# A two-layer decoder trunk: the FFN's up products summed in PSUM chains with operands from one half of SBUF, and f's sums of the down projection made by adding transfers

## The chip, the cores and the metric

The kernel runs on one core of a Trainium2 chip. The time is the device time of one execution in microseconds (us). TensorE (PE) multiplies, VectorE (DVE), ScalarE (ACT) and GpSimd (POOL) do elementwise work, SyncE (SP) and the other queues issue transfers. A matmul here takes a stationary 128x128 operand and a moving 128x512 operand from SBUF and adds into a PSUM bank of 128x512 float32.

## The reference

Two layers, each a token mixer of three groups (MLA, GLA, RWKV-7) and a gated ConvFFN, on a sequence of 1024 tokens of width 1024:

```python
def conv_ffn(h, w_up, conv_w, conv_b, w_down):
    u = jnp.einsum('bsd,df->bsf', h, w_up)
    u = lax.conv_general_dilated(u, conv_w[:, None, :].astype(u.dtype), window_strides=(1,),
                                 padding=[(CONV_WIDTH - 1, 0)],
...
    gate, val = u[..., :D_FF], u[..., D_FF:]
    return jnp.einsum('bsf,fd->bsd', jax.nn.silu(gate) * val, w_down)

for l in range(DEPTH):
    h = rms_norm(x, ln1_g[l])
    p = jnp.einsum('bsd,dp->bsp', h, w_in[l])
...
    x = x + jnp.einsum('bsm,md->bsd', y, w_out[l])
    x = x + conv_ffn(rms_norm(x, ln2_g[l]), ffn_w_up[l], ffn_conv_w[l], ffn_conv_b[l], ffn_w_down[l])
return rms_norm(x, final_g)
```

The lines left out make y from p by the three mixers. D_FF is 2816, so the up projection makes 2 x 22 tiles of 128 rows (22 of gate, 22 of value), and the down projection reads f = silu(gate) * val in 22 tiles.

## The kernel before

Every float32 operand is held as two parts, a high one that ACT rounds and a low one that DVE or POOL subtracts (`split`, L1270); `mm3` (L97 issues) makes three matmuls of such a pair. Both FFN projections use a 2x2 block scheme with seven products in place of eight.

**Up projection.** For each j of 22 (one gate tile and one value tile) there are seven products p = 1, 2, 6, 5, 3, 7, 4, each 12 matmuls of 128x512 (four blocks k, three matmuls each): 1848 matmuls per layer. The stationary operand of a product is an item: `up_item` (L1354) builds the four weight sums (tiles S12, S34, on POOL after the first j's) and splits the chosen part into the tile `wr`, which lives in one of seven left slots, `RING`. The moving operands are the tokens' block sums: B11 (p=1), B21 (2), T2 (6), T1 (5), B22 (3), T3 (7), T4 (4). B11 to B22 lie in the pool `bp` and T3 in `wp`, both on the right side of SBUF; T4 (tiles T_m1, T_kb00 and so on) in left slots. So all products but p=4 take the weights from the left and the tokens from the right. `product` (L1482) gives each product its own bank, by turns from `aps` and `bps` (tiles psa and psr). `evac` (L1448) empties each bank: ACT copies p=1 and 5, DVE adds a copied term for 2, 6, 3, 7 and 4, and POOL adds the last term to the gate's and the value's second half. Then `taps` (L1439) applies the three conv taps to the gate (ug) and the value (uv): one ACT instruction and two DVE instructions of 1023 and 1022 columns, all from SBUF to SBUF; ACT makes the SiLU, DVE multiplies gate and value, and f[j] is stored to DRAM (`fdr`).

**Down projection.** 11 q's (two tiles of f and of w_down each, loaded as the eight quarters of `R`, L1523) in groups of 3, 4 and 4. Each q has seven products in the order 1, 2, 5, 6, 3, 7, 4, summed over the q's of a group in PSUM: 924 matmuls per layer. Before products, DVE makes the sums of f's quarters (R[0..3]) and of the weights' quarters (R[4..7]) in four steps, sum_a to sum_d (L1551 to L1564), and splits (`down_split`, L1568; ACT the high, DVE the low part) into `de` units; `down_product` adds each finished bank to an accumulator (L1604 wide, L1607 narrow).

**Around them.** The out projection (w_out rows k = 0 to 7, `wout_w`) runs before the up projection, tile of tokens by tile; its weights are split into left slots except k = 7. `up_norm` (L1274) turns each token tile into B11, B21 (first four tiles) or B22, T1, T2, T3 (last four). The order on each engine is set by a scheduler from the order of the code, so every engine runs its queue in a fixed order.

## Time and profile before

| | |
|---|---|
| median of 3 runs | 2751.63 us (2751.45 to 2755.01) |
| profiled execution, own time | 2754.38 us |
| its span in the profile | 2752.6 us |
| mean granted TensorE clock | 0.974 of full speed |
| PE busy | 2650.9 us, 96% of the span, 13586 matmuls |
| DVE busy | 1867.2 us (68%) |
| POOL busy | 1125.0 us (41%) |
| ACT busy | 1080.8 us (39%) |

The profiled execution is 2.8 us above the median. Stretches below are counted in us from the start of the span. Layer 1's out projection starts near 590, its up projection near 690 and its down projection near 1155; layer 2 repeats these places some 1372 us later. A matmul's listed duration overlaps the next one's; the pace is read from start to start. The granted clock of a window is its mean over the window, of the two levels 1.2 and 2.4 GHz (0.5 and 1.0).

### The profile page before, as it was taken

The page shows a single profiled execution, that of the slowest core. Times are in us where ns is not written, and L with a number is a line of the kernel's source. Part 1 is how long each engine was busy: PE and PEld are TensorE (multiplying, and loading weights), DVE is VectorE, ACT ScalarE, POOL GpSimd, SP SyncE. Part 2 cuts the span into 40 slices and gives each one's busy share as a digit, 9 for nine tenths or more (in the row PEclk, how much of TensorE's full clock was granted, in tenths as well). Part 3 has the DMA queues.
Part 4 walks back from the last instruction along what each step waited for, and adds up shares of the span by engine and source line. Part 5 has one row for each costly group of instructions (what it writes and reads, how often), then busy time and mean ns, then how long its engine had stood idle before and what let it go on. Part 6 is the DMA issues. An engine that isn't in the chain of part 4 may idle for free. (4 is left out here: it accounts for less than half of the span.)

```text
span 2752.6 us, 35450 instructions
## 1 busy us (share of the span) xinstructions
PE 2650.9 (96%) x13586; PEld 2135.5 (78%) x13586; DVE 1867.2 (68%) x2470; ACT 1080.8 (39%) x1764; POOL 1125.0 (41%) x915
## 2 busy tenths in 40 slices
PE   8999999999899999999899999999998999998998
...
GB/s 128 31 31 62 64 61 38 45 126 138 52 86 77 84 77 77 237 100 101 58 45 31 31 70 73 51 32 57 121 135 54 77 81 81 80 74 260 85 84 62
DMA packets 237050, 224.11 MB, mean 81 GB/s; under 512 B 39288, under 2 KB 187216, under 8 KB 236880
## 3 DMA queue, kind: packets, MB, share of 16 engines
...
## 5 line engine op out<-in xcount | busy, mean ns | idle before, releaser
L97 PE MATMUL psb<-hh,wh 128*128 128x512 f32 (+2 forms) x704 | 267.3, 381 | 6.5 <-ACT acc L748 3.8
L1443 DVE SCALAR_TENSOR_TENSOR acc<-ug,convc,acc 128x1023 f32<-128x1023 f32 x88 | 190.6, 2166 | 122.2 <-ACT acc L1441 122.1
L97 PE MATMUL psb<-hl,wh 128*128 128x512 f32 (+2 forms) x704 | 270.7, 385 | 0.8 <-DVE hl L208 0.8
L97 PE MATMUL psb<-hh,wl 128*128 128x512 f32 (+2 forms) x704 | 270.1, 384 | 0.8 <-POOL wl L258 0.8
L97 PE MATMUL psa<-B,wr_m 128*128 128x512 f32 x744 | 187.7, 402 | 1.9 <-DVE uv L1471 1.9
L97 PE MATMUL psr<-B,wr_m 128*128 128x512 f32 x744 | 185.6, 397 | 0.0
L97 PEld LDWEIGHTS psa<-B,wr_m 128*128 128x128 f32 x744 | 142.6, 192 | 37.5 <-DVE uv L1471 2.7
L254 POOL TENSOR_TENSOR ws<-ws,pcol 128x1024 f32<-128x1024 f32 x36 | 70.4, 1958 | 243.0 <-DMA ws<-in_w_in 242.8
L97 PEld LDWEIGHTS psr<-B,wr_m 128*128 128x128 f32 x744 | 140.6, 189 | 34.2 <-DVE s_va L1460 0.3
L97 PEld LDWEIGHTS psb<-hh,wh 128*128 128x128 f32 (+1 forms) x704 | 132.9, 189 | 36.5 <-issue 4.9
L97 PEld LDWEIGHTS psb<-hh,wl 128*128 128x128 f32 (+1 forms) x704 | 133.2, 189 | 33.3 <-issue 10.5
L97 PEld LDWEIGHTS psb<-hl,wh 128*128 128x128 f32 (+1 forms) x704 | 133.1, 189 | 29.2 <-issue 5.4
L258 POOL TENSOR_TENSOR wl<-ws,wh 128x1024 fp32r<-128x1024 f32 (+1 forms) x40 | 91.0, 2276 | 105.9 <-ACT wh L256 70.9
L1441 ACT ACTIVATE acc<-ug,convc 128x1024 f32<-128x1024 f32 x44 | 54.8, 1246 | 202.1 <-POOL ug L1466 202.1
L1443 DVE SCALAR_TENSOR_TENSOR acc<-uv,convc,acc 128x1023 f32<-128x1023 f32 x88 | 120.0, 1364 | 8.0 <-ACT acc L1441 6.7
L1272 DVE TENSOR_TENSOR wr_m<-wu_m,wr_m 128x512 fp32r<-128x512 f32 x88 | 120.9, 1375 | 0.2 <-ACT wr_m L1271 0.2
L1272 POOL TENSOR_TENSOR wr_sg<-S_va,wr_sg 128x512 fp32r<-128x512 f32 x40 | 58.0, 1449 | 120.0 <-ACT wr_sg L1271 116.3
L1468 ACT ACTIVATE acc<-acc 128x1024 f32<-128x1024 f32 x44 | 46.7, 1062 | 149.1 <-DVE acc L1443 149.1
L1271 ACT ACTIVATE de_m<-R 128x1024 fp32r<-128x1024 f32 x59 | 61.9, 1052 | 109.9 <-PE psb L97 50.8
L1364 POOL TENSOR_TENSOR S_va<-wu_m 128x512 f32<-128x512 f32 x42 | 57.0, 1358 | 114.8 <-issue 107.6
L256 ACT ACTIVATE wh<-ws 128x1024 fp32r<-128x1024 f32 (+2 forms) x44 | 43.7, 993 | 150.7 <-PE psb L97 141.4
L97 PE MATMUL psb<-de 128*128 128x512 f32 x348 | 94.6, 394 | 0.0
...
## 6 DMA issues: line engine op xcount, KB each, us to landing
...
```

Source lines behind the costliest of these rows:

```text
L97: pe.matmul(o, lhsT=l, rhs=r, start=first, stop=last, skip_group_check=on)
L254: eng.tensor_tensor(ws, ws, g.rearrange("p (k o) -> p k o", o=1).to_broadcast([128, K, M]), ALU.mult)
L256: act.activation(wh, ws, AF.Copy)
L258: eng.tensor_tensor(wl, ws, wh.bitcast(F32), ALU.subtract)
L1271: act.activation(d[0], s, AF.Copy)
L1272: eng.tensor_tensor(d[1], s, d[0].bitcast(F32), ALU.subtract)
L1364: eng.tensor_tensor(X[:, 0], v[:, 0:4], v[:, 4:8], ALU.add)
L1441: act.activation(a, u, AF.Identity, scale=conv[:, 2, jj:jj + 1], bias=conv[:, 3, jj:jj + 1])
L1443: dve.scalar_tensor_tensor(a[:, d:T], u[:, 0:T - d], conv[:, 2 - d, jj:jj + 1], a[:, d:T], ALU.mult, ALU.add)
L1468: act.activation(a, a, AF.Silu)
```

## The change

- **Chains.** P6 adds onto P1's bank, P7 onto P6's, P4 onto P7's, and P3 onto P5's; P2 has its own. Between them ACT copies the bank's state out for p = 1, 6, 5 and 4, DVE adds once for p = 2, 7 and 3, and POOL's two adds are gone. From j = 3 on the taps' result stands in PSUM (`bigps`) and not in SBUF. The final product gate * val is made in two halves, the first with a factor of -1, so that f's first half is stored negated and f's sums in the down projection become additions.
- **Halves.** Items of p = 2, 6, 5, 7 and 3 live in five slots RG on the right side, beside B21, T2, T1, B22 and T3; items of p = 1 and 4 in three left slots, beside B11 (moved to left slots kb01, kb11, va01, va11) and T4. The rows k = 5 and 6 of w_out take RG in place of those left slots, and the first token tile's out projection does k = 0 to 4 of both halves first.
- **Small moves.** `raw` has two buffers, the subtraction of B11 from a token tile is four DVE instructions of 256 columns in place of two of 512, and p = 7 comes before p = 3.
- **Down projection.** For q in the second and third group f's sums are made by adding DMAs on the POOL queue (`plus`, 64 in all, 128x512 each); DVE keeps the weights' sums. In the first group the low parts of p = 1 are split by POOL. The finished banks are subtracted.

```diff
-            if k < 7:
+            if k < 5:
                 woh[k], wol[k] = (slot(o, [128, D], F32R, "wo") for o in WOA[k])
+            elif k < 7:
+                woh[k], wol[k] = (RG[:, 2 * k - 10 + n].rearrange("p a k c -> p (a k c)") for n in range(2))
...
-        B11, B21, T2, T1, B22 = (pair(n) for n in ("B11", "B21", "T2", "T1", "B22"))
+        RG = bp.tile([128, 5, 2, 4, 128], F32R, tag="RG", name="RG")
+        B21, T2, T1, B22 = (pair(n) for n in ("B21", "T2", "T1", "B22"))
+        B11 = [[slot(t, [128, 2, 512], F32R, "B11") for t in ts] for ts in (("kb01", "kb11"), ("va01", "va11"))]
...
+        def less(x, tk):
+            for part in B11:
+                for n in range(2):
+                    xn = x[:, 2 * n:2 * n + 2]
+                    dve.tensor_tensor(xn, xn, part[n][:, :, tk].bitcast(F32), ALU.subtract)
...
-        RING = ("m4", "m5", "sg", "m9", "m8", "kb11", "m3")
+        RING = ("m4", "m5", "sg")
...
-            c = slot(RING[rn % len(RING)], [128, 2, 4, 128], F32R, "wr")
+            n = made[up]
+            c = RG[:, (n + 4) % 5] if up else slot(RING[n % 3], [128, 2, 4, 128], F32R, "wr")
...
-            if p == 2:
+            if p in (1, 5, 6):
+                act.activation(s[:, {1: 0, 5: 1, 6: 2}[p]], ps, AF.Copy)
+            elif p == 2:
                 tmp[j, "g"] = wp.tile([128, T], F32, tag="wl", name="ug")
                 dve.tensor_tensor(tmp[j, "g"][:, H0], ps, s[:, 0], ALU.add)
-            elif p == 6:
-                dve.tensor_tensor(s[:, 2], ps, s[:, 0], ALU.add)
-            elif p == 5:
-                act.activation(s[:, 1], ps, AF.Copy)
+            elif p == 7:
+                tmp[j, "v"] = wp.tile([128, T], F32, tag="wl", name="uv")
+                dve.tensor_tensor(tmp[j, "v"][:, H1], ps, s[:, 1], ALU.add)
             elif p == 3:
                 u = tmp[j, "g"]
                 dve.tensor_tensor(u[:, H1], ps, s[:, 2], ALU.add)
-                pool.tensor_tensor(u[:, H1], u[:, H1], s[:, 1], ALU.add)
-                a = tmp[j, "a"] = taps(u, j, dict(tag="x", bufs=2))
-                act.activation(a, a, AF.Silu)
+                a = tmp[j, "a"] = xr.tile([128, T], F32, tag="x", name="acc", bufs=2)
+                act.activation(a, taps(u, j, a if j < 3 else bigps()), AF.Silu)
+            else:
+                u = tmp[j, "v"]
+                act.activation(u[:, H0], ps, AF.Copy)
+                b = taps(u, NF + j, lp.tile([128, T], F32, tag="raw", name="b", bufs=2) if j < 3 else bigps())
                 a = tmp[j, "a"]
+                dve.scalar_tensor_tensor(a[:, H0], a[:, H0], -1.0, b[:, H0], ALU.mult, ALU.mult)
+                dve.tensor_tensor(a[:, H1], a[:, H1], b[:, H1], ALU.mult)
                 nc.sync.dma_start(out=fdr[j], in_=a)
...
+            elif p == 2 or p == 5:
+                banks[j, p] = banks["big"][:, H1] if (j, p) == (2, 2) else bps()
+            else:
+                banks[j, p] = banks[j, {6: 1, 7: 6, 4: 7, 3: 5}[p]]
+            ps, new = banks[j, p], p in (1, 2, 5)
             c = items.pop((j, p))
             for k in range(4):
-                mm3(ps, (c[:, 0, k], c[:, 1, k]), rhs(p, k), k == 0, k == 3)
+                mm3(ps, (c[:, 0, k], c[:, 1, k]), rhs(p, k), new and k == 0, k == 3, not new)
...
+        def plus(o, x):
+            pool.dma_start(out=o, in_=x, accum_op=ALU.add)
+
+        def sum_a(R, q):
+            if q in groups[0]:
+                dve.tensor_tensor(R[:, 2], R[:, 2], R[:, 3], ALU.add)
+            else:
+                plus(R[:, 2], fdr[2 * q + 1][:, H1])
+                plus(R[:, 0], fdr[2 * q][:, H1])
+            dve.tensor_tensor(R[:, 6], R[:, 4], R[:, 6], ALU.subtract)
+
+        def sum_b(R, q):
+            if q in groups[0]:
+                dve.tensor_tensor(R[:, 2], R[:, 2], R[:, 0], ALU.add)
+            else:
+                plus(R[:, 2], fdr[2 * q][:, H0])
+                plus(R[:, 1], R[:, 2])
+            dve.scalar_tensor_tensor(R[:, 6], R[:, 6], -1.0, R[:, 7], ALU.mult, ALU.subtract)
...
-            split(dent[q, p], two(draw[q], *OPS[p]), dve)
+            split(dent[q, p], two(draw[q], *OPS[p]), pool if p == 1 and q in groups[0] else dve)
```

sum_c and sum_d follow the same pattern: on DVE, f's part for the first group only, and one 128x512 instruction for the weights.

**Place 1: PE in the middle of layer 1's up projection.** psa and psr are banks, the numbers buffers. Before, one j's products stand one behind the other (P1, P2, P6, P5, P3, and P7's first matmul), each in a bank of its own:

```order
L97 MATMUL psr_8559<-B11_4913,wr_m4_8429 128x512 x12
L97 MATMUL psa_8577<-B21_4914,wr_m5_8447 128x512 x12
L97 MATMUL psr_8595<-T2_4915,wr_sg_8470 128x512 x12
L97 MATMUL psa_8618<-T1_4916,wr_m9_8487 128x512 x12
L97 MATMUL psr_8635<-B22_4917,wr_m8_8510 128x512 x12
L97 MATMUL psa_8658<-T3_4960,wr_kb11_8529 128x512
```

Now, from the end of P6 of a j (bank psa_6503) to its P7 in the same bank (last row):

```order
L97 MATMUL psr_6559<-T1_4919,RG_4916 128x512 x12
L97 MATMUL psr_6657<-B21_4917,RG_4916 128x512 x6
L97 MATMUL psa_6639<-B11_kb01_4921,wr_m4_6518 128x512
L97 MATMUL psa_6639<-B11_va01_4923,wr_m4_6518 128x512
L97 MATMUL psr_6657<-B21_4917,RG_4916 128x512 x4
L97 MATMUL psa_6639<-B11_kb01_4921,wr_m4_6518 128x512 x2
L97 MATMUL psa_6639<-B11_va01_4923,wr_m4_6518 128x512
L97 MATMUL psa_6639<-B11_kb01_4921,wr_m4_6518 128x512
L97 MATMUL psa_6639<-B11_kb11_4922,wr_m4_6518 128x512
L97 MATMUL psa_6639<-B11_va11_4924,wr_m4_6518 128x512
L97 MATMUL psa_6639<-B11_kb11_4922,wr_m4_6518 128x512 x2
L97 MATMUL psa_6503<-T3_4963,RG_4916 128x512
```

The next j's P2 (psr_6657) and P1 (psa_6639) moved in between, so that 32 matmuls stand between P6 and P7 of one bank.

**Place 2: DVE at the start of layer 1's down projection.** acc is an accumulator, R a loaded q, de a unit. Before, from the first finished wide bank (psb) to the first narrow ones (psa, psr):

```order
L1604 TENSOR_TENSOR acc_m1_8978<-psb_9064,acc_m1_8978 128x1024
L1563 TENSOR_TENSOR R_8856<-R_8856 128x512
L1560 TENSOR_TENSOR R_8856<-R_8856 128x2x512
L1564 TENSOR_TENSOR R_8856<-R_8856 128x512
L1272 TENSOR_TENSOR de_m7_9105<-R_8856,de_m6_9104 128x1024
L1604 TENSOR_TENSOR acc_kb00_8980<-psb_9084,acc_kb00_8980 128x1024
L1443 SCALAR_TENSOR_TENSOR acc_9001<-ug_8874,convc_511,acc_9001 128x1022
L1607 TENSOR_TENSOR acc_m1_8978<-psa_9119,acc_m1_8978 128x512
L1607 TENSOR_TENSOR acc_m1_8978<-psr_9120,acc_m1_8978 128x512
```

And now:

```order
L1643 TENSOR_TENSOR acc_m1_8806<-acc_m1_8806,psb_8894 128x1024
L1585 TENSOR_TENSOR R_8876<-R_8876 128x512
L1589 TENSOR_TENSOR R_8719<-R_8719 128x512
L1593 SCALAR_TENSOR_TENSOR R_8719<-R_8719 128x512
L1597 TENSOR_TENSOR R_8742<-R_8742 128x512
L1602 TENSOR_TENSOR R_8742<-R_8742 128x512
L1598 SCALAR_TENSOR_TENSOR R_8742<-R_8742 128x512
L1603 SCALAR_TENSOR_TENSOR R_8742<-R_8742 128x512
L1646 TENSOR_TENSOR acc_m1_8806<-acc_m1_8806,psa_8954 128x512
L1646 TENSOR_TENSOR acc_m1_8806<-acc_m1_8806,psr_8955 128x512
```

Seven sums of the first and second group's q's moved ahead of the narrow banks' subtraction; P2's matmuls now come before P1's on PE.

**Place 3: DVE in layer 1's third group, between the splits of p = 6.** Before:

```order
L1556 TENSOR_TENSOR R_9046<-R_9046 128x512
L1557 TENSOR_TENSOR R_9046<-R_9046 128x512
L1563 TENSOR_TENSOR R_8895<-R_8895 128x512
L1560 TENSOR_TENSOR R_8895<-R_8895 128x2x512
L1564 TENSOR_TENSOR R_8895<-R_8895 128x512
L1272 TENSOR_TENSOR de_m3_10098<-R_8895,de_sg_10097 128x1024
L1556 TENSOR_TENSOR R_9055<-R_9055 128x512
L1557 TENSOR_TENSOR R_9055<-R_9055 128x512
L1563 TENSOR_TENSOR R_9046<-R_9046 128x512
L1560 TENSOR_TENSOR R_9046<-R_9046 128x2x512
L1564 TENSOR_TENSOR R_9046<-R_9046 128x512
L1272 TENSOR_TENSOR de_m7_10158<-R_9046,de_m6_10157 128x1024
```

And now:

```order
L1646 TENSOR_TENSOR acc_kb10_8834<-acc_kb10_8834,psa_10022 128x512
L1598 SCALAR_TENSOR_TENSOR R_8701<-R_8701 128x512
L1603 SCALAR_TENSOR_TENSOR R_8701<-R_8701 128x512
L258 TENSOR_TENSOR wl_10104<-ws_10098,wh_10102 128x640
L1646 TENSOR_TENSOR acc_kb10_8834<-acc_kb10_8834,psr_10023 128x512
L1646 TENSOR_TENSOR acc_kb01_8836<-acc_kb01_8836,psa_10050 128x512
L258 TENSOR_TENSOR wl_10177<-ws_10172,wh_10175 128x1024
L1277 TENSOR_TENSOR de_va01_10003<-R_8885,de_kb11_10002 128x1024
L1646 TENSOR_TENSOR acc_kb01_8836<-acc_kb01_8836,psr_10051 128x512
L1277 TENSOR_TENSOR de_m7_10007<-R_8701,de_m6_10006 128x1024
L1277 TENSOR_TENSOR de_m5_10015<-R_8742,de_m4_10014 128x1024
```

f's sums left the stretch; the splits of p = 6 follow each other with only evacuations and the next layer's weight split (L258) among them.

## Rows read from the trace of the kernel before

**Rows 1.** Windows of 50 us: busy time and instructions per engine, granted clock, DMA share.

```profile
700.00:750.00 50.00, 42.49 (x170) 32.78 (x169) 44.60 (x41) 20.70 (x31) 34.23 (x19) 0.93 0.18 53
750.00:800.00 50.00, 45.10 (x183) 35.89 (x182) 45.92 (x38) 21.39 (x32) 35.66 (x22) 0.93 0.24 79
1000.00:1050.00 50.00, 50.00 (x215) 39.85 (x214) 37.49 (x32) 20.45 (x29) 36.23 (x25) 1.00 0.21 67
1150.00:1200.00 50.00, 40.92 (x153) 30.47 (x152) 48.30 (x59) 18.52 (x18) 0.00 (x0) 0.90 0.63 221
1300.00:1350.00 50.00, 42.44 (x170) 32.98 (x169) 40.53 (x45) 14.45 (x15) 5.08 (x2) 0.93 0.17 53
...
2670.00:2720.00 50.00, 50.00 (x217) 40.46 (x216) 44.04 (x51) 17.87 (x19) 0.00 (x0) 1.00 0.00 1
```

**Rows 2.** Timeline of PE in layer 1's up projection: start, us, instructions, idle before.

```profile
821.82 1.52 PE L97 MATMUL psr<-T_kb,wr_m 128*128 128x512 f32 x6
823.18 2.97 PE L97 MATMUL psa<-B,wr_m 128*128 128x512 f32 x12
825.99 2.97 PE L97 MATMUL psr<-B,wr_m 128*128 128x512 f32 x12
```

**Rows 3.** Timeline of PE in the in projection, first and last of 18 matmuls.

```profile
62.06 0.40 PE L97 MATMUL psb<-hh,wh 128*128 128x512 f32 x1
...
65.94 0.39 PE L97 MATMUL psb<-hh,wl 128*128 128x512 f32 x1
```

**Rows 4.** Timeline of PE, waits in the first products of the up projection, both layers.

```profile
707.06 0.49 PE L97 MATMUL psr<-T,wr_m 128*128 128x512 f32 x1 [2.68 <-ACT T L1271]
710.41 0.79 PE L97 MATMUL psa<-T,wr_m 128*128 128x512 f32 x1 [2.85 <-ACT T L1271]
...
738.31 0.70 PE L97 MATMUL psa<-T,wr_sg 128*128 128x512 f32 x2 [0.84 <-DVE ug L1465]
...
770.21 3.33 PE L97 MATMUL psa<-T,wr_m 128*128 128x512 f32 x7 [4.90 <-DVE uv L1471]
...
2142.03 3.32 PE L97 MATMUL psa<-T,wr_m 128*128 128x512 f32 x7 [4.90 <-DVE uv L1471]
```

**Rows 5.** The page's costliest groups, DVE's taps: total, mean ns, idle before.

```profile
L1443 DVE SCALAR_TENSOR_TENSOR acc<-ug,convc,acc 128x1023 f32<-128x1023 f32 x88 | 190.6, 2166 | 122.2 <-ACT acc L1441 122.1
...
L1443 DVE SCALAR_TENSOR_TENSOR acc<-uv,convc,acc 128x1023 f32<-128x1023 f32 x88 | 120.0, 1364 | 8.0 <-ACT acc L1441 6.7
```

**Rows 6.** Timeline of DVE, one stretch at the start of the down projection.

```profile
1157.68 1.21 DVE L1272 TENSOR_TENSOR de_m<-R,de_m 128x1024 fp32r<-128x1024 f32 x1
1158.82 1.21 DVE L1604 TENSOR_TENSOR acc_kb<-psb,acc_kb 128x1024 f32<-128x1024 f32 x1
1159.95 1.26 DVE L1443 SCALAR_TENSOR_TENSOR acc<-ug,convc,acc 128x1022 f32<-128x1022 f32 x1
1161.14 0.68 DVE L1607 TENSOR_TENSOR acc_m<-psa,acc_m 128x512 f32<-128x512 f32 x1
1161.74 0.67 DVE L1607 TENSOR_TENSOR acc_m<-psr,acc_m 128x512 f32<-128x512 f32 x1
```

**Rows 7.** Timeline of ACT in the up projection.

```profile
742.66 1.25 ACT L1441 ACTIVATE acc<-ug,convc 128x1024 f32<-128x1024 f32 x1 [3.49 <-POOL ug L1466]
...
749.22 1.23 ACT L1441 ACTIVATE acc<-uv,convc 128x1024 f32<-128x1024 f32 x1
750.35 0.57 ACT L1454 ACTIVATE s_va<-psb 128x512 f32<-128x512 f32 x1
```

**Rows 8.** Timeline of PE at the down projection's start, the two longest waits.

```profile
1158.95 1.22 PE L97 MATMUL psb<-de_m,de_m 128*128 128x512 f32 x2 [2.91 <-DVE de_m L1272]
...
1175.30 2.08 PE L97 MATMUL psb<-de_va,de_va 128*128 128x512 f32 x4 [3.39 <-DVE de_va L1272]
```

**Rows 9.** Timeline of PE in layer 1's third group, the two longest waits.

```profile
1330.40 0.73 PE L97 MATMUL psb<-de_m,de_m 128*128 128x512 f32 x2 [2.76 <-DVE de_m L1272]
...
1335.14 0.51 PE L97 MATMUL psr<-de_m 128*128 128x512 f32 x1 [2.38 <-DVE acc_kb L1607]
```

**Rows 10.** Out projection's start, timelines of POOL and PE.

```profile
592.50 2.34 POOL L1171 TENSOR_TENSOR wo<-wos,wo 128x1024 fp32r<-128x1024 f32 x1 [3.25 <-DMA ydr<-rcb]
...
594.89 1.20 PE L97 MATMUL psr<-wo,yhl_m 128*128 128x512 f32 x4 [1.76 <-POOL wo L1171]
```

**Rows 11.** The line of POOL's own transfers (128 KB each): us from issue to landing.

```profile
DMA to landing us min/median/max: 2.1/2.3/4.1
```

145 lines of the change are left out of this document (72 added, 73 removed).

## The prediction

> **What bounds the kernel now.** First the busy shares: PE is busy 96% of the span, so the time is PE's matmuls plus the places where PE waits or runs at the lower clock. The number of matmuls does not change (1848 up and 924 down per layer), so the change can only alter their pace and those places. The windows of 50 us [rows 1] show both: the steady up projection holds 215 matmuls at full clock, while 700 to 750 holds 170, 750 to 800 holds 183, 1150 to 1200 holds 153 and 1300 to 1350 holds 170. At 50/215 = 0.233 us each, the four windows lose 10.5, 7.4, 14.4 and 10.5 us. Part is the wait itself; the rest is a granted clock of 0.93 or 0.90, which costs 7 to 10% of a window, 3.5 to 5 us. The waits' releasers [rows 4, 8, 9] are ACT's T splits, then DVE; DVE is busy 45 to 48 of 50 us in three of these windows [rows 1]. Layer 2 repeats the first three places (the wait of 4.90 us stands at 770.21 and at 2142.03 [rows 4]), but not the last: 2670 to 2720 holds 217.
>
> **Pace of the up projection.** With weights on the left and tokens on the right, twelve matmuls take 825.99 - 823.18 = 2.81 us, 234.2 ns each; p=4, both on the left, takes (823.18 - 821.82)/6 = 226.7 [rows 2]. The in projection, both on the right, takes (65.94 - 62.06)/17 = 228.2 [rows 3]. So neither the side nor the tile, but having both operands on one side goes with the quicker pace, in two places that share nothing else. The change puts all seven products on one side. Six products x 12 x 22 = 1584 matmuls per layer gain about 234.2 - 227.9 = 6.3 ns, taking a middle of the two quick rows: 10.0 us per layer, **-20 us**. Its ends are 0 (the cause is another) and -24 (226.7 throughout). The rows k=5 and 6 of w_out go the other way: RG on the right against the out projection's tokens on the left, 2 x 3 x 2 x 8 = 96 matmuls per layer at +6.3 ns, **+1 us** in all.
>
> The Trainium skill ("TensorE: Matmul & The Clock Gate", Step-by-step) says that PE has two independent SBUF read ports, one for the streamed operand and one for the weights, so that loading weights takes no bandwidth from the running matmul. By that rule this term would be 0 and the sum would stand 20 us higher. Rows 2 and 3 speak against it: the pace differs by 6 to 7 ns with the operands' places. It is a rival below.
>
> **First products.** PE waits 2.68 and 2.85 us for T1 and T2 of the last token tile [rows 4]. In the new order P5(0) stands whole ahead of P6(0), raw has a second buffer, but the subtraction takes four instructions in place of two. Following the queues I find about 3.9 us of waits where 5.5 stood: **-3 us** for two layers, ends 0 and -11 (both gone).
>
> **Second and third j.** From 737 to 771 PE waits 0.84 and 4.90 us and twice under a microsecond for DVE's evacuations [rows 4], 6.9 in all, with about 3.4 us of lower clock behind them (the second window's 7.4 lost less the 4.90 in it leaves 2.5; by its clock it is 3.5). DVE is saturated there, its taps stretched: an instruction that takes 1364 ns for the value takes 2166 for the gate, which POOL's work overlaps [rows 5]. The change takes two 128x512 adds per j off DVE (0.60 each from start to start [rows 6]) and two off POOL, and P4 needs only ACT's copy. Behind the 4.90 us DVE had 0.60 x 2 x 3 = 3.6 us for the three j's less, and the path through POOL's add goes too. Following the new queues, nothing above 0.4 us of waiting is left; DVE's slack is 1 to 2 us. I take 9 of 10.3 us per layer: **-18 us**, ends -6 and -21.
>
> **The chains themselves.** Each chain adds a wait: P7 may not start before ACT has copied P6's state, P4 not before DVE's add, P6 not before the copy of P1, P3 not before P5's. Place 1 of the order puts 32 matmuls between P6 and P7, 32 x 0.228 = 7.3 us; the copy takes 0.57 [rows 7], queued behind one item split at the most, so some 6 us are spare. P7 to P4 has 3 to 4 us spare, P1 to P6 some 4. Per j PE needs 84 x 0.228 = 19.2 us; ACT's work is about 9 and DVE's about 10, so queues are short. Cost 0 in the steady state. Item slots, five in place of seven, give each right-hand item four products, 11 us, for a split of 0.6 + 1.4: hidden also. If that cover fails, it is the rival below.
>
> **Start of the down projection.** PE waits 2.91 and 3.39 us and five times less [rows 8], 9.8 in all, at a clock of 0.90. DVE does 0.3 us per q less here (the p=1 splits go to POOL), but in the new order (place 2) it makes seven sums ahead of the narrow banks' subtraction. Adding starts (0.60 for 512 columns, 1.14 for 1024, 1.19 for a tap [rows 6]) from the end of P4: the first wide bank is subtracted at 16.8 us, the narrow ones at 22.4, and the first low part for P6 at 32.3. PE, having 36 + 36 matmuls and then needing these, waits 0.8 + 4.2 + 6.1 = 11.1 us, where 9.8 stood; clock as before. **+2 us** for two layers, ends -16 and +12.
>
> **Second and third group.** Four sums per q of 512 columns leave DVE, about 2.2 us per q. Where PE is the bound that is worth nothing. In layer 1's third group PE waits 2.76, 2.38 and twice less for DVE, 7.5 us with the clock's 3 [rows 9, 1]; between 1305 and 1335 f's sums take some 6.4 of DVE's time, all ahead of the late splits (place 3). Following the new queue I find the splits of p=6 at most 2 us late. **-5 us**, ends +6 and -10.5. Layer 2 has nothing there to gain [rows 1]. The price is 32 adding transfers per layer on POOL's queue, each waiting for the last one's landing at two places per q. The nearest row lands 128 KB in 2.3 us at the median and 4.1 at most [rows 11]; these carry 256 KB, and I take 3 to 5 us. From the split of p=5 to that of p=6 there are 11 us or more, so they are hidden unless they take twice that.
>
> The Trainium skill ("SBUF — State Buffer", Two separate sides) warns that a transfer issued by POOL stands still while certain DVE operations keep POOL from writing its descriptors; it names copies from SBUF to SBUF, and no run here shows it for these subtractions. Were it so, the adds would come late, which is the third rival.
>
> **Start of the out projection.** POOL's low parts of w_out (2.34 us each) start when its last transfer of y has landed [rows 10]; k=5 and 6 now write RG, which is freed late, so three such parts stand there in place of one. The first tile's other rows, k = 0 to 4 of both halves (30 matmuls, 6.9 us), cover most. **+2 us** for two layers, ends -2 and +8.
>
> **Sum.** -20 + 1 - 3 - 18 + 0 + 2 - 5 + 2 = -41 us. Against the profiled execution's own 2754.4 that is 2713; it lies 2.8 above the median of the runs, and the median 2751.6 gives 2711. I forecast **2711 us**.
>
> **Rivals.**
> (1) *The pace is not a matter of sides*: 234 ns stays. For it speaks the rule of two ports; against it both quick rows. 2711 + 20 = **2731**.
> (2) *The third j stays late*: DVE's slack of 1 to 2 us at 737 to 771 is used up by its contention with POOL [rows 5], so half of the 18 us stays. **2720** to 2729.
> (3) *The adding transfers are late.* In each of two groups of two layers PE would wait for a split of p=6 or 3; with 4 us and a clock drop of 3.4 at each it is 4 x 7.4 = 30 less the 5 not gained: **2741** to 2746.
> (4) *The chains bind, and it is slower than before.* ACT's queue is in order: if the copy of P6 stands behind a SiLU or Identity (1.25 us [rows 7]) that itself waits for DVE's taps, it comes a whole DVE round later. This decides once the copy is more than 6 us late; then each of the 38 steady j's loses that excess. From 1.1 us of excess on (38 x 1.1 = 42) the kernel is slower; at 1.5 us it is 2711 + 57 = **2768**. Against it: in the new queue SiLU stands behind the copies of its j, and ACT is busy 20 of 50 us [rows 1].
> (5) *The change doesn't do what it says*, for instance the scheduler's waits come earlier than the order shows: 2745 to 2752.
>
> **How the numbers follow.** Forecast 0.54 (2696 to 2722 by its own ends), (1) 0.12, (2) 0.12, (3) 0.10, (4) 0.08, (5) 0.04. Leaving out (4), (5) and the upper half of (3), about 0.17, the range reaches from 2692 to 2740. A measurement of this kernel can tell about 0.2%, 5.5 us, from no change: faster means below 2746, slower above 2757. Faster: 0.54 + 0.12 + 0.12 + 0.10 less a little = 0.86; same: 0.05; slower: 0.09.
>
> **What would show it.** In the new profile the steady windows should hold 219 matmuls in 50 us (215 would be rival 1); 750 to 800 should be full at clock 1.00, without a wait for a DVE add; the down projection's start should still hold about 150 to 160 in its window, with waits for narrow banks and P6's split; 1300 to 1350 nearly 215. A line of waits for ACT's copies in every j would be rival 4, and waits of DVE or ACT on POOL's transfers rival 3.

## The result

The changed kernel takes 2736.0 us at the median of four runs (2732.9 to 2738.1), beside 2751.5 for the kernel before: a ratio of 0.9937, interval 0.9922 to 0.9952. It is faster by 15.5 us, where 41 were forecast. Its profiled execution took 2732.9 (span 2731.1), 21.5 less than that of before. All ratios here are of fast runs alone; one execution of e4_own_banks below, of 6192 us, is not among them. By place, in us, each stage from the start of its first matmul to the start of its last, in the two traces:

| place | before | after | difference | forecast |
|---|---|---|---|---|
| out projection, layers 1 and 2 | 105.2, 105.2 | 111.8, 112.0 | +13.4 | +3 |
| up and down projection, layer 1 | 693.8 | 672.7 | -21.1 | -44 |
| up and down projection, layer 2 | 684.8 | 670.7 | -14.0 | (both layers) |
| last product to layer 2's first | 9.1 | 12.4 | +3.3 | 0 |
| last product to the end | 10.7 | 14.4 | +3.8 | 0 |
| layer 2's in projection and mixers | 563.2 | 557.7 | -5.5 | 0 |

The rest, -1.3, lies ahead of layer 1's out projection.

The windows of the changed kernel (length, busy us and instructions of PE, weight loads, DVE, ACT, POOL, then granted clock, DMA share, GB/s) answer to [rows 1]:

```profile
700.00:750.00 50.00, 43.87 (x188) 35.41 (x186) 45.50 (x49) 23.87 (x38) 30.08 (x20) 0.93 0.19 53
750.00:800.00 50.00, 46.83 (x201) 37.08 (x200) 42.18 (x40) 23.98 (x36) 31.21 (x19) 1.00 0.33 106
1000.00:1050.00 50.00, 50.00 (x220) 40.97 (x219) 32.51 (x36) 24.62 (x37) 26.27 (x20) 1.00 0.27 85
1100.00:1150.00 50.00, 45.06 (x185) 35.66 (x184) 37.70 (x42) 22.87 (x28) 10.76 (x6) 0.93 0.82 287
1150.00:1200.00 50.00, 42.03 (x171) 33.48 (x170) 42.76 (x52) 17.58 (x18) 6.95 (x8) 0.93 0.72 202
1300.00:1350.00 50.00, 49.03 (x213) 39.64 (x212) 39.92 (x48) 16.70 (x17) 12.03 (x9) 1.00 0.54 123
```

The steady window holds 220 matmuls (215 before), 750 to 800 holds 201 at full clock (183), layer 1's third group holds 213 (170). So the steps inside the up and down projection are there. What ate them stands in PE's waits (start, us, instruction, idle before it and its releaser), at the start of the out projection, in the first products and at the start of the down projection, in this order:

```profile
592.62 1.20 PE L97 MATMUL psr<-RG,yhl_m 128*128 128x512 f32 x4 [0.53 <-POOL RG L1172]
595.82 1.22 PE L97 MATMUL psr<-wo,yhl_m 128*128 128x512 f32 x2 [2.00 <-ACT wo L1171]
598.24 2.07 PE L97 MATMUL psr<-wo,yhl_m 128*128 128x512 f32 x4 [1.21 <-POOL wo L1172]
...
714.69 0.53 PE L97 MATMUL psr<-T,RG 128*128 128x512 f32 x1 [4.61 <-ACT T L1276]
716.36 5.06 PE L97 MATMUL psr<-T,RG 128*128 128x512 f32 x11 [1.13 <-POOL T L1277]
...
753.32 0.72 PE L97 MATMUL psa<-B_kb,wr_m 128*128 128x512 f32 x2 [1.12 <-POOL wr_m L1277]
...
1143.70 0.80 PE L97 MATMUL psb<-de_kb 128*128 128x512 f32 x1 [4.41 <-ACT acc L1492]
1156.85 0.50 PE L97 MATMUL psa<-de_sg 128*128 128x512 f32 x1 [2.23 <-DVE acc_m L1646]
1167.26 1.22 PE L97 MATMUL psb<-de 128*128 128x512 f32 x2 [5.74 <-DVE de L1277]
...
1323.41 0.50 PE L97 MATMUL psb<-de_va,de_kb 128*128 128x512 f32 x1 [0.96 <-DVE de_va L1277]
```

The first three were one wait of 1.76 in layer 1 [rows 10], and in layer 2, where they stand again, nothing above 0.41; the two for T are 5.7 us where 5.5 stood [rows 4]; second and third j wait 3.2 us in all (6.9 before): the 4.90 us at the third j are gone [rows 4]; the down projection waits 12.8 us with one of 0.42 that is not shown (9.8 before [rows 8]); the third group waits 0.96 (7.5 [rows 9]).

### The profile page after: what moved, and what is told of

Same layout as the page of the kernel before. It is cut to its first block, busy times and chain, and to the rows that moved or that the text cites. A ratio compares the mean times of both kernels' runs of the same rounds, so it can differ in the third digit from the quotient of the medians.

```text
span 2731.1 us, 35559 instructions
## 1 busy us (share of the span) xinstructions
PE 2629.2 (96%) x13586; PEld 2134.9 (78%) x13586; DVE 1697.6 (62%) x2418; ACT 1127.0 (41%) x1860; POOL 1032.0 (38%) x897
## 3 DMA queue, kind: packets, MB, share of 16 engines
q8 instruction: 107, 1.75, 0.3%
## 4 chain that ended last, share of the span: by engine, by line
PE 79%; DVE 9%; DMA 3%; ACT 3%; issue 3%; POOL 2%; SPq 0%; POOLq 0%; DVEq 0%; ACTq 0%
PE psb L97 26%; PE psr L97 19%; PE psa L97 18%; PE psa L1146 2%; DMA R<-in_ffn_w_down 1%; PE psa L1135 1%; PE psr L896 1%; PE psr L862 1%; PE psr L807 1%; DVE Ttmp L699 1%; DVE Tb L701 1%; PE psa L503 1%; PE psr L900 1%; PE psr L838 1%; PE psr L494 1%
## 5 line engine op out<-in xcount | busy, mean ns | idle before, releaser
L97 PE MATMUL psr<-B,RG 128*128 128x512 f32 x1032 | 254.1, 391 | 1.0 <-ACT s_va L1481 0.5
L97 PE MATMUL psa<-T,RG 128*128 128x512 f32 x1008 | 247.4, 391 | 1.0 <-ACT RG L1276 1.0
L97 PEld LDWEIGHTS psr<-B,RG 128*128 128x128 f32 x1032 | 193.4, 188 | 44.7 <-ACT s_va L1481 1.5
L1277 POOL TENSOR_TENSOR RG<-S_m,RG 128x512 fp32r<-128x512 f32 x86 | 120.2, 1398 | 274.1 <-ACT RG L1276 239.3
L97 PEld LDWEIGHTS psa<-T,RG 128*128 128x128 f32 x1008 | 190.0, 189 | 42.7 <-ACT RG L1276 1.8
L1276 ACT ACTIVATE RG<-S_m 128x512 fp32r<-128x512 f32 x176 | 110.9, 630 | 225.3 <-PE psa L97 120.3
L97 PE MATMUL psr<-T,RG 128*128 128x512 f32 x528 | 137.7, 403 | 11.2 <-ACT T L1276 9.2
L1469 DVE SCALAR_TENSOR_TENSOR psb<-uv,convc,psb 128x1023 f32<-128x1023 f32 x76 | 97.7, 1285 | 55.5 <-ACT psb L1467 54.5
L97 PEld LDWEIGHTS psr<-T,RG 128*128 128x128 f32 x528 | 102.0, 194 | 35.8 <-ACT T L1276 10.1
L258 POOL TENSOR_TENSOR wl<-ws,wh 128x1024 fp32r<-128x1024 f32 (+1 forms) x40 | 91.2, 2281 | 98.0 <-ACT wh L256 62.9
L97 PE MATMUL psb<-de 128*128 128x512 f32 x384 | 109.0, 400 | 15.2 <-DVE de L1277 8.1
L1469 DVE SCALAR_TENSOR_TENSOR psb<-ug,convc,psb 128x1023 f32<-128x1023 f32 x76 | 97.5, 1283 | 25.2 <-ACT psb L1467 24.2
```

The source lines that it names most:

```text
L97: pe.matmul(o, lhsT=l, rhs=r, start=first, stop=last, skip_group_check=on)
L258: eng.tensor_tensor(wl, ws, wh.bitcast(F32), ALU.subtract)
L1276: act.activation(d[0], s, AF.Copy)
L1277: eng.tensor_tensor(d[1], s, d[0].bitcast(F32), ALU.subtract)
L1469: dve.scalar_tensor_tensor(a[:, d:T], u[:, 0:T - d], conv[:, 2 - d, jj:jj + 1], a[:, d:T], ALU.mult, ALU.add)
```

## The experiments

Beside the experiments the kernel before took 2754.9 to 2756.2 us, each time the median of 7 to 17 runs. Each kernel is given as its ratio to that; the changed kernel is 0.9937, which is 2738 there.

### The ends of the sum: one part at a time

**e2_k7_first** loads and splits w_out's row k=7 ahead of 5 and 6:

```diff
-        for k in range(5, 8):
+        for k in (7, 5, 6):
```

> The changed kernel with w_out's rows loaded and split in the order k = 7, 5, 6 in place of 5, 6, 7. Theory: at the out projection's start PE waits for k=7 because its staging buffer is the one of k=5, which is free only after POOL's low part of k=5, and that waits for RG; with k=7 first its load and split do not stand behind RG. Waits of 3.7 us at 592 to 599 and the low clock behind them go to 1.3 us or less, 4 to 5 us per layer: 2736 becomes 2727. Rival: POOL's three parts of 2.35 us set the start whatever the order: 2734 to 2737.

0.9958 (0.9944 to 0.9972), 2742.5 us. No gain: the out projection waits 2.76, 1.72 and 1.21 us. The row that stands third, now k=6, waits for its staging buffer as k=7 did (its load is issued at 592.11, when POOL's low part of the first ends), so the order is not the lever.

**e3_dve_sums** makes f's sums on DVE in all groups, without adding transfers:

```diff
-            if q in groups[0]:
-                dve.tensor_tensor(R[:, 2], R[:, 2], R[:, 3], ALU.add)
-            else:
-                plus(R[:, 2], fdr[2 * q + 1][:, H1])
-                plus(R[:, 0], fdr[2 * q][:, H1])
+            dve.tensor_tensor(R[:, 2], R[:, 2], R[:, 3], ALU.add)
...
```

> The changed kernel with all of f's sums on DVE and no adding transfers. Theory: they are worth something only in layer 1's third group, where PE waits for DVE again, 7 us and 3 us of low clock: 2736 becomes 2744 to 2747; the down projection's start stays as it is, and layer 2 too. Rival: the adding transfers cost as much as they give, by late splits or by slowing DVE and the loads: 2733 to 2737.

0.9945 (0.9927 to 0.9963): the same as the changed kernel. In layer 1's third group three waits stand, of 0.93, 0.63 and 1.75 us, and the down projection of layer 1 is 3 us longer; that of layer 2 is not. So the adding transfers are worth some 3 us in the trace, and most of what layer 1's third group lost before went with the rest of the change.

**e4_own_banks** undoes the chains in PSUM (each product of the up projection in its own bank, the sums back on DVE and POOL) and keeps the places, the five slots and the taps in PSUM:

```diff
-            if p in (1, 5, 6):
-                act.activation(s[:, {1: 0, 5: 1, 6: 2}[p]], ps, AF.Copy)
+            if p in (1, 5):
+                act.activation(s[:, {1: 0, 5: 1}[p]], ps, AF.Copy)
+            elif p == 6:
+                dve.tensor_tensor(s[:, 2], ps, s[:, 0], ALU.add)
...
```

> The changed kernel with the chains undone: every product has its own bank, DVE adds five times and POOL twice per j; halves, slots and taps in PSUM stay. Theory: the chains are worth what they take off DVE and POOL in the second and third j, so the waits there grow from 3.2 to some 7 us per layer with low clock behind them, and the steady state keeps 220 matmuls in 50 us: 2736 becomes 2748 to 2752. Rival: the taps in PSUM and the second buffer of raw did that and the chains are worth nothing: 2736. Rival: the chains' waits cost PE time: below 2733.

0.9992 (0.9979 to 1.0004): all of the gain is gone. Its windows and its longest wait near the third j:

```profile
750.00:800.00 50.00, 42.23 (x172) 33.59 (x171) 43.62 (x40) 20.69 (x30) 34.11 (x23) 0.93 0.23 75
...
900.00:950.00 50.00, 50.00 (x221) 41.17 (x220) 33.13 (x41) 23.39 (x33) 30.54 (x25) 1.00 0.24 73
```

```profile
757.13 0.80 PE L97 MATMUL psa<-T_m,wr_sg 128*128 128x512 f32 x1 [5.62 <-DVE s_va L1483]
```

The steady windows are as quick without chains (221). At the second and third j the waits are 8.0 us in both layers, where the changed kernel has 3.2 and 3.6, and 6.8 us at the lower clock follow them; 172 matmuls stand in place of 201. But not all of the 15 us is shown to be the chains'. Between the two profiles, 17.2 us apart, the up and down projections of layer 1 differ by only 1.3 us (674.0 in place of 672.7: shorter waits and less low clock at the first products, at the down projection's start and a quicker steady part give the rest back) and those of layer 2 by 7.5 (678.2 in place of 670.7). Layer 2's out projection is 2.3 us longer, and 6.1 lie in its in projection and mixers, whose instructions are the same. So by the stages that they touch, the chains are worth some 9 us, and the rest stays open.

### The late start of the out projection

ACT and POOL at that place in the changed kernel:

```profile
586.68 2.01 ACT L1171 ACTIVATE RG<-wos 128x1024 fp32r<-128x1024 f32 x2 [0.40 <-DMA x<-in_x]
...
594.71 1.06 ACT L1171 ACTIVATE wo<-wos 128x1024 fp32r<-128x1024 f32 x1 [4.80 <-DMA wos<-in_w_out]
```

```profile
587.84 4.73 POOL L1172 TENSOR_TENSOR RG<-wos,RG 128x1024 fp32r<-128x1024 f32 x2 [0.84 <-DMA ydr<-o]
595.84 2.35 POOL L1172 TENSOR_TENSOR wo<-wos,wo 128x1024 fp32r<-128x1024 f32 x1 [3.28 <-ACT wo L1171]
```

RG lies on bytes that the attention's v and P hold until its last product (585.8), so k=5 and 6 are split from 586.7 on, where the kernel before had them done at 576.4. (That the bytes are the same follows from where the tiles are placed; the trace shows the order in time.) The third row's load waits for the staging buffer that POOL's first low part still reads.

**e7_staging** stages k=7 elsewhere and gives one low part to DVE:

```diff
-            ws = slot("m9", [128, D], F32, "wos") if k < 5 else wp.tile([128, D], F32, tag="ws", name="wos")
+            ws = slot("m9", [128, D], F32, "wos") if k < 5 else wp.tile([128, D], F32, tag="ws" if k < 7 else "wh", name="wos")
...
-                pool.tensor_tensor(wol[k], ws, woh[k].bitcast(F32), ALU.subtract)
+                (dve if k == 6 else pool).tensor_tensor(wol[k], ws, woh[k].bitcast(F32), ALU.subtract)
```

> The changed kernel, where w_out's row block k=7 is staged in another buffer than k=5 (its load need not wait for POOL's low part of k=5) and k=6's low part is made on DVE. Theory 'the late start of the out-projection is the staging buffer and POOL's queue': its stage goes from 112.1 and 112.2 us to 107 to 109 in both layers, 2736 to 2728 (2724 to 2732). Rival 'the place of the weights itself, free only at the end of the attention, is late': 111 to 112 stay, 2736 (2733 to 2740).

0.9929 (0.9915 to 0.9943), the stage 111.6 and 110.1 us: nothing that can be told. The rows show why:

```profile
591.25 3.33 POOL L1172 TENSOR_TENSOR RG<-wos,RG 128x1024 fp32r<-128x1024 f32 x1
```

```profile
589.92 2.46 DVE L1172 TENSOR_TENSOR RG<-wos,RG 128x1024 fp32r<-128x1024 f32 x1 [6.92 <-ACT RG L1171]
```

Beside each other the two engines took 3.33 and 2.46 us for what takes 2.38 and 1.2 alone, and PE waited 3.77 us in one piece. They seem to take turns: DVE's ends 1.1 us after POOL's part before it (588.91 to 591.29), POOL's second 2.2 us after DVE's.

**e10_low_dve** gives all three low parts to DVE (`dve if k > 4 else pool`):

> The changed kernel with k=7 of w_out staged in another buffer and the low parts of k=5 to 7 all on DVE (POOL is left out of it, since beside each other the two took 2.46 and 3.33 us for what takes 1.2 and 2.4 alone). Theory 'the out-projection starts late since k=5 and 6 can be split only after the attention's last product, and then three parts of 2.4 us follow each other on POOL': DVE is through some 3 us earlier, the stage 112 to 106 us in both layers, 2738 to 2728 (2724 to 2733). Rival 'the split's place decides, whoever makes it': 111 to 112 stay, 2738 (2734 to 2742).

0.9899 (0.9882 to 0.9916), the stage 105.5 and 109.0. DVE, and what PE still waits:

```profile
590.14 1.23 DVE L1172 TENSOR_TENSOR wo<-wos,wo 128x1024 fp32r<-128x1024 f32 x1 [5.88 <-DMA ydr<-rcb]
591.28 2.35 DVE L1172 TENSOR_TENSOR RG<-wos,RG 128x1024 fp32r<-128x1024 f32 x2
```

```profile
592.56 1.67 PE L97 MATMUL psr<-RG,yhl_m 128*128 128x512 f32 x6 [0.41 <-DVE RG L1172]
```

In layer 1, 3.7 us of waits became 0.41, no lower clock follows, and the stage is as long as in the kernel before. The staging is that of e7, which gained nothing, so the place of the low parts made the difference: POOL's queue after a late release was the cause. Layer 2 stays 3.7 us longer than in the kernel before: ACT splits RG there only at 1945.34, behind another instruction of its queue, PE waits 1.03 us for that and 0.72 for DVE's low part, and 3.4 us at the lower clock follow.

### The two ends of the down projection

In the changed kernel ACT scales the first row of the next layer only when the last product is done, and the first output rows come as late:

```profile
1364.09 1.33 ACT L234 ACTIVATE xn_m<-acc_va,ss 128x512 f32<-128x512 f32 x2 [6.02 <-PE psb L97]
...
2712.77 0.63 ACT L218 ACTIVATE o<-acc_m 128x512 f32<-128x512 f32 x1 [10.41 <-DVE acc_m L1643]
2715.07 0.63 ACT L218 ACTIVATE o<-acc_va 128x512 f32<-128x512 f32 x1 [1.57 <-PE psb L97]
```

The list of buffers for split f and weights is one longer (UNITS has ten entries, LEFT six). Counted through, the last product now holds m6 and m7, which the next layer's first rows want, and both pairs of ws and wh, which six of the eight output rows want.

**e8_end_buffers** gives these rows other buffers:

```diff
-                return slot(("m6", "m7", "m4", "m5")[i % 4], [128, D], F32, "xn")
+                return slot(("m4", "m5", "m6", "m7")[i % 4], [128, D], F32, "xn")
...
-                o = wp.tile([128, D], F32, tag=("ws", "wh", "wl")[i % 3], name="o")
+                op, t = ((wp, "wl"), (lp, "raw"), (wp, "wl"), (lp, "raw"), (xr, "x"), (xr, "x"), (wp, "ws"), (wp, "wh"))[i]
+                o = op.tile([128, D], F32, tag=t, name="o", bufs=2)
```

> The changed kernel with other buffers at the two ends of the down projection: the normalized rows 0 and 1 between the layers in m4 and m5, not m6 and m7, which the last product still reads; the output rows in wl, raw, x and only last in ws and wh, which the last product still reads. Theory 'the ends are late because the first rows wait for buffers that the last product holds': between the layers 12.4 to 9 us, the end 14.4 to 10.5, 2736 to 2729 (2726 to 2732). Rival 'they are late because the last sums are': both stay, 2736 (2733 to 2740).

0.9912 (0.9900 to 0.9925). Between the layers 9.2 us, at the end 10.7: both as in the kernel before. The same row of ACT now stands before the last product's end (1370.9):

```profile
1365.37 0.72 ACT L234 ACTIVATE xn_m<-acc_va,ss 128x512 f32<-128x512 f32 x1
```

### What sets the pace

**e1_places** measures the pace by itself, on zeros: 13 tiles of 16 KB across SBUF, each as weights with each as tokens, 12 products a pair:

> Only matmuls of 128x512 on zeros, none of the reference's work: 13 tiles of 16 KB per partition lie one behind the other in SBUF, and 12 matmuls back to back take their weights from tile i and the moving operand from tile j, for all 169 pairs. No other engine works beside them. Theory (halves): 227 to 228 ns from start to start where i and j lie on one side of a boundary in the middle of SBUF, 234 where they lie on two sides. Rival (independent ports): 227 for all pairs. Rival (another pattern in the addresses, or other engines' accesses): no such blocks, or 227 for all pairs although the kernel shows 234.

226.7 ns for all 169 pairs. So the halves, as such, are not the cause. All these tiles lie at multiples of 16 KB from one another, which the tiles of the kernels don't.

**e5_shift_before** and **e6_shift_after** put a 32-byte tile first at the right end of SBUF, before and after the change, so that all tiles on both sides start at a multiple of 64 bytes:

```diff
+    padp = ctx.enter_context(tc.tile_pool(name="padp", bufs=1, side="right"))
+    padp.tile([128, 8], F32, name="pad8")
     wp = wstack.enter_context(tc.tile_pool(name="wp0", bufs=2, side="right", reuse_waits="tile"))
```

> The kernel before, with a 32-byte tile placed first at the right end of SBUF, so that all tiles there lie 32 bytes lower; nothing else. In the kernel before, left tiles start at multiples of 64 bytes and right tiles 32 bytes off, so that the up products with weights on one side and tokens on the other differ in that phase; with the shift all agree. Theory 'the pace is the phase of the two addresses': the steady part of the up projection goes from 215-216 matmuls per 50 us to 220 without moving a tile to another side, -19 us over two layers: 2733 (2728 to 2738). Theory 'the pace is the half of SBUF': 215-216 stay, 2752 (2749 to 2755). Theory 'neither, the change took work of other engines away': 2752 as well.

> The changed kernel with the same 32-byte tile. Its up products have equal phase already, so by the theory of phases nothing moves: 2736 (2733 to 2740), with p=1 at 233-234 ns and the other products at 227-229 ns as they are. Should the absolute phase count (right tiles 32 bytes off a multiple of 64), the out-projection's RG with yhl goes from 234 to 227 ns, 0.7 us per layer, and nothing else: 2735.

The kernel before: 0.9993 (0.9982 to 1.0004), products with weights and tokens on two sides still at 233.3 ns. The changed kernel: 0.9906 (0.9888 to 0.9924), some 8 us less, against both expectations: p=1, which lies on the left as it did and took 232.8 ns on average, takes 228.4, the products around it go from 228.1 to 227.2, and the window from 850 to 900 holds 222:

```profile
850.00:900.00 50.00, 50.00 (x222) 41.35 (x221) 29.67 (x34) 24.41 (x37) 24.48 (x18) 1.00 0.30 95
```

**e9_pairs** takes pairs at the kernels' own addresses, first alone and then beside DVE, ACT or POOL:

> A measurement of the pace by itself, without the reference's work (the output is zeros): triples of 128x512 products with weights and tokens at the addresses that the up projection uses: left/right with phases 0/32 (wr, rm), left/right with equal phase (wr, rn), right/right (rg, rm: 32/32; rg, rn: 32/0), left/left (wr, tm; wr, be; ws, be), 24 in a row each; first with no other engine at work, then while DVE, ACT or POOL works on tiles left or right. Theory 'the pace comes from the two operands alone': wr with rm 234 ns and same-half pairs 227 ns in the first part already. Rival 'other engines' accesses make it': 227 ns for all in the first part, 234 where another engine works, and then for cross pairs or unequal phases only.

The first part, with no other engine at work (24 products a row; the difference of two starts, over 24, is the pace):

```profile
46.55 5.78 PE L105 MATMUL ps<-rm,wr 128*128 128x512 f32 x24
52.17 5.62 PE L105 MATMUL ps<-rn,wr 128*128 128x512 f32 x24
57.63 5.76 PE L105 MATMUL ps<-rn,rg 128*128 128x512 f32 x24
63.23 0.40 PE L105 MATMUL ps<-tma,wr 128*128 128x512 f32 x1
...
65.08 0.61 PE L105 MATMUL ps<-tmc,wr 128*128 128x512 f32 x2
...
68.71 0.39 PE L105 MATMUL ps<-bea,wr 128*128 128x512 f32 x1
```

rm with wr (two sides; tokens 160 bytes beyond the weights, modulo 256) takes 234 ns; rn with wr (two sides, 0) 227.5; rn with rg (both right, 96) 233; and the parts beside other engines repeat these numbers wherever PE doesn't wait. So the pace comes from the two operands' addresses, not from other engines. The last three rows show p=1's case: behind a row at other addresses the first eight products take (65.08 - 63.23)/8 = 231 ns, though their own distance is 0, and the next sixteen (68.71 - 65.08)/16 = 227. In the changed kernel p=1 stands between products of the other side, 160 bytes off (modulo 256): after each change of side the first eight products or so take 224 to 236 ns, and then 227 comes. After the shift the sides lie 128 off, and 227 comes from the second product on. That is what e6 gained; why the settling depends on the distance stays open.

**e12_offsets** varies only the distance between the two addresses, with both tiles left and then on two sides:

> The pace by itself, without the reference's work (the output is zeros): weights in one tile, tokens in another whose address differs from that of the weights by 0, 32, 64, 128, 256, 384, 512 and 1024 bytes beyond a multiple of 1024, 36 products of 128x512 for each, first with both tiles left, then with the tokens at the right end. Theory 'the distance modulo 512 bytes decides': 227 ns for 0, 512 and 1024, 233 to 234 for 32, 64, 128, 256 and 384, the same on both sides. Rival 'modulo 64 decides': 227 ns for all but 32. Rival 'the halves': all 227 in the first part, all 234 in the second.

The second part, where tokens lie 0, 32, 64, 128, 256, 384, 512 and 1024 bytes off (psa to psh):

```profile
87.96 8.32 PE L86 MATMUL psa<-rr,wr 128*128 128x512 f32 x36
96.12 8.57 PE L86 MATMUL psb<-rr,wr 128*128 128x512 f32 x36
104.52 8.41 PE L86 MATMUL psc<-rr,wr 128*128 128x512 f32 x36
112.78 8.53 PE L86 MATMUL psd<-rr,wr 128*128 128x512 f32 x36
121.14 8.34 PE L86 MATMUL pse<-rr,wr 128*128 128x512 f32 x36
129.32 8.55 PE L86 MATMUL psf<-rr,wr 128*128 128x512 f32 x36
137.71 8.34 PE L86 MATMUL psg<-rr,wr 128*128 128x512 f32 x36
145.89 8.32 PE L86 MATMUL psh<-rr,wr 128*128 128x512 f32 x36
```

The last 24 of each row take 226.7, 233.3, 228.9, 232.7, 226.7, 233.3, 226.7 and 226.7 ns, and the same to 0.1 ns with both tiles left. 256 is as good as 0, 128 and 384 are as bad as 32: the distance modulo 256 bytes fits all eight, and no theory that stood before the run had it. In the kernel before, weights and tokens on two sides differed by 160 bytes modulo 256, as rm and wr do, after the 32-byte shift by 128, which is slow too; the change put both on one side, where they agree.

**e13_shift416_before** shifts the right side of the kernel before by 416 bytes, so that both sides agree modulo 512 (and takes the smaller scratch of the changed kernel, to have room):

> The kernel before with a 416-byte tile at the right end of SBUF in place of none, so that weights on the left and tokens on the right have equal addresses modulo 512 (480 and 64 before); no tile changes its half; the scratch of the software queue is 8 KB as in the changed kernel, to make room. Theory 'distance modulo 512': the up projection's steady windows go from 215-216 to 220 or more products per 50 us, 2755.5 to 2736 (2731 to 2741). Theory 'halves': 2755 (2751 to 2759).

0.9974 (0.9963 to 0.9984). Every product of the up projection takes 226.7 ns (p=7, which now waits, and p=4 behind it take a little more), and yet its stage takes 451.7 us where 452.3 stood. PE, at the place where it now waits in each j:

```profile
855.70 3.02 PE L97 MATMUL psa<-T,wr_kb 128*128 128x512 f32 x12 [0.23 <-DVE ug L1460]
...
875.40 3.01 PE L97 MATMUL psr<-T,wr_kb 128*128 128x512 f32 x12 [0.23 <-DVE ug L1460]
```

From p=7 to p=7 it is 19.70 us; in the kernel before it is 84 x 234 ns = 19.66. PE waits for DVE's sum of p=2. Five j's later, DVE from one such sum (first row) to the next (last row), and POOL between:

```profile
953.56 0.68 DVE L1460 TENSOR_TENSOR ug<-psr,s_va 128x512 f32<-128x512 f32 x1
...
957.00 0.68 DVE L1274 TENSOR_TENSOR wr_m<-S_va,wr_m 128x512 fp32r<-128x512 f32 x1
...
964.60 2.27 DVE L1445 SCALAR_TENSOR_TENSOR acc<-ug,convc,acc 128x1023 f32<-128x1023 f32 x1 [3.75 <-ACT acc L1443]
...
973.23 0.68 DVE L1460 TENSOR_TENSOR ug<-psa,s_va 128x512 f32<-128x512 f32 x1
```

```profile
957.81 1.29 POOL L1366 TENSOR_TENSOR S_va<-wu_m 128x512 f32<-128x512 f32 x1 [3.02 <-issue]
...
962.00 1.29 POOL L1468 TENSOR_TENSOR ug<-ug,s_va 128x512 f32<-128x512 f32 x1
```

The sum stands in DVE's queue behind the taps of the last j (from 964.60); these wait for ACT, and ACT (963.33) for POOL's add (962.00). That add does not wait for DVE's sum of p=3, which ended 3.7 us earlier (958.28): it stands in POOL's queue behind the next item's weight sums, and POOL begins these 0.13 us after DVE's split of the last ones ends (957.68), so in each of the nine j's from 839 to 997; the profile names no releaser. The split stands in DVE's queue behind the sum of p=2. So the loop goes from DVE over POOL and ACT back to DVE, without PE. It takes 19.7 us, and the quicker pace of PE only shows it. In the kernel before the same loop comes round in 19.7 us too, as long as PE's own 84 products take there. The 8.7 us that e13 is quicker lie elsewhere: between the profiles, 10.9 us apart, 5.3 are in the two down projections, 2.9 in layer 2's in projection and mixers and 1.3 in the out projections.

**e15_taps_in_sbuf** and **e16_taps_in_psum** ask what freed the changed kernel of that loop. The first takes its taps back to SBUF, the second gives taps in PSUM to the kernel of e13:

```diff
-                act.activation(a, taps(u, j, a if j < 3 else bigps()), AF.Silu)
+                act.activation(a, taps(u, j, a), AF.Silu)
...
```

```diff
-            a = xr.tile([128, T], F32, **tag, name="acc")
+            a = bigps() if jj % NF > 2 else xr.tile([128, T], F32, **tag, name="acc")
...
```

> The changed kernel with the convolution's taps accumulated in SBUF for every j, as in the kernel before, and not in PSUM from j=3 on. Theory 'taps in PSUM keep DVE early enough for the quick pace': a wait comes once per j, the steady windows fall from 220 to 214-216, 10 us per layer, 2738 to 2757 (2750 to 2762). Rival 'the chains' lighter DVE work is enough': 219-220 stay, 2738 (2734 to 2744).

> The kernel before with the 416-byte shift of e13 and the taps accumulated in PSUM from j=3 on; its own banks, buffers and order stay. Theory 'the taps in SBUF held it': no wait per j, steady windows from 214-216 to 221, some 10 us per layer, 2747.5 to 2730 (2724 to 2736). Rival 'another part of the change did it (order of p=7 and p=3, five slots, fewer adds)': windows stay at 214-216, 2747 (2743 to 2751).

e15: 0.9916 (0.9892 to 0.9939), windows of 219 and 220 and no wait: with the chains the taps may lie in SBUF. e16: 0.9871 (0.9839 to 0.9904), 2722.8 us, windows of 222 and no wait per j. So either relief of the loop is enough, fewer adds on DVE and POOL or taps in PSUM, and e13, which has neither, shows that one is needed. The kernel before, with a shift and taps in PSUM, is faster than the changed kernel. A group of taps in e13, and in e16 (total us, mean ns, idle before):

```profile
L1445 DVE SCALAR_TENSOR_TENSOR acc<-ug,convc,acc 128x1023 f32<-128x1023 f32 x88 | 189.4, 2152 | 128.9 <-ACT acc L1443 128.8
```

```profile
L1445 DVE SCALAR_TENSOR_TENSOR psb<-ug,convc,psb 128x1023 f32<-128x1023 f32 x76 | 97.2, 1279 | 15.3 <-ACT psb L1443 15.3
```

The taps of the gate take 1279 ns in place of 2152. The Trainium skill ("SBUF — State Buffer", SBUF: two separate sides) says that a DVE operation with two inputs in SBUF and a POOL operation that reads SBUF exclude each other for a whole instruction. These rows agree: with the sum in PSUM one input is left in SBUF, and the stretching by POOL is gone. In e13 the taps of the value that no POOL instruction overlaps take 1272 ns, about as short as all of e16's in PSUM, 70 of whose gate taps lie beside POOL's work for most of their time (1279).

### All together

**e11_all** joins e6, e8 and e10; **e14_all416** takes the shift by 416 bytes in place of 32.

> The changed kernel with the 32-byte shift, the buffers at the two ends and the low parts on DVE together. If the three add up (-6, -7 and -10 on the 2738 that the changed kernel is worth on this chip): 2715 (2710 to 2722). If the low parts give nothing: 2725 (2721 to 2730). It should be under both kernels in either case.

> The changed kernel with the buffers at the two ends and the low parts on DVE as in e11_all, and a shift by 416 bytes in place of 32. In e11_all 624 products are left whose weights and tokens differ by 384 bytes modulo 512, here 240 that differ by 256. By the theory 'distance modulo 512' some 400 products gain 6 to 7 ns, 2.5 us: 2709 to 2707 (2703 to 2711). By 'modulo 64' nothing: 2709 (2705 to 2713).

e11: 0.9834 (0.9815 to 0.9854), 2709.2 us. The three parts add up: 0.0031, 0.0025 and 0.0038 under the changed kernel make 0.0094, and it is 0.0103. e14: 0.9807 (0.9792 to 0.9823), 2700.5 us; by the ratios 36 us under the changed kernel and 53 under the kernel before. Against e11 the intervals overlap a little; the gain of the out projection shows in the trace, from 105.6 and 109.1 us to 104.5 and 106.4. Its steady window from 800 to 850 holds 222 matmuls, and every product in it takes 226.7 ns.

## Why the prediction was right or wrong

The direction was right, the size was not: -15.5 us (-21.5 between the profiles) where -41 was forecast, just inside the range. The steps that failed are the start of the out projection and w_out's place, taken at +3 and measured at +13.4, and the two ends, which no term named and which cost +7.0; "nothing above 0.4 us of waiting is left" at the second and third j and the first products follow with some 4 and 3. That the time lies near rival 1's 2731 is chance: the pace came.

- **Pace, -20.** The size was right: 84 products per j at 229.0 ns where 234.2 stood, 0.44 us per j, 9.6 us per layer if all 22 j's are counted. The reason was wrong. Not the side decides but the distance of the two addresses modulo 256 (e1, e9, e12); the two quick rows that I took as evidence [rows 2, 3] had both operands on one side and so, here, at equal addresses. Rival 1 was neither right nor wrong: sides are not the cause, and the pace came nevertheless. The Trainium skill's rule of two independent read ports ("TensorE: Matmul & The Clock Gate", Step-by-step) would make the pace the same for every pair; the 226.7 and 233.3 ns of e12 differ from it, and the measurement decides.
- **The chains, 0.** By themselves, in the steady part, that holds: PE waits nowhere in the steady windows, so rival 4 is out, and e4 is no quicker there than by one matmul in 50 us. But the step took each term alone, and the pace is worth nothing in the up projection unless the loop over DVE, POOL and ACT gets shorter (e13). That condition was not in the sum. The loop would have been found by adding up what stands between two sums of p=2, from DVE through POOL and ACT back to DVE, and not only PE's own 84 products.
- **Second and third j, -18.** Right in kind, too large: 6.9 us of waits became 3.2 in layer 1 and 3.6 in layer 2, and the lower clock behind them is gone; some 14 us for both. The step that failed is "nothing above 0.4 us of waiting is left": waits of 1.13, 0.43, 0.50 and 1.13 us are left in layer 1.
- **First products, -3.** Nothing came: 4.61 and 1.13 us where 2.68 and 2.85 stood. ACT's split waits for DVE's subtraction, whose four pieces take 4.1 us for the last token tile (709.80 to 713.90) where two took 1.8. No run takes them back.
- **Start of the down projection, +2.** 12.8 us of waits in layer 1 where 11.1 were forecast, right in kind. The 4.41 us for ACT's SiLU, which reads a bank that the down projection wants, were not in it.
- **Second and third group, -5.** Better: 0.96 us in place of 7.5 and the clock at 1.00, nearly 10 us. The adding transfers from DRAM land in 4.7 us at the median, inside the 3 to 5 taken (3.3 to 8.2 over all 64); ACT waits for one of them once, 3.2 us at 1227, and PE does not wait there, so rival 3 is out. But the reason given, f's sums leaving DVE, carries only some 3 us of it (e3); no run ties the rest to a part of the change.

```profile
R<-fdr POOLq DMA_DIRECT2D x48, 256.0 KB, 4.7
```

- **Start of the out projection, +2, and w_out's place, +1.** The worst term: +13.4. The late release of RG was seen, and its three low parts on POOL; the third row's load, which waits for a staging buffer that POOL still reads, was not, nor the clock behind the waits: 0.50 from 598 to 602 with 8 matmuls, where the kernel before has 1.00 and 19. The cover of 6.9 us was taken to hide most of three low parts of 2.34 us, 7.0 in all; it had no room for the 4.80 us that ACT waits for the load between the second and the third.
- **The two ends, 0.** +7.0 that no term named (e8). One entry more in each of two lists of buffers moved the later users, and those that the last product holds are then the ones that the next rows want.
- **Layer 2's in projection and mixers, -5.5.** These instructions are the same in both kernels, but the scheduler orders them anew with each edit; over the fifteen profiles of whole kernels here the stretch took 557 to 566 us. No run ties this to a part of the change, and it stays open. Without it the profiles differ by 16.0.

Between the forecast and the profile without that stretch lie 25 us: 10.4 at the out projection, 7.0 at the ends, 3 and 4 in the products of the last token tile and of the second and third j. The other misses nearly cancel.
